# A gated feed-forward up projection by seven block products in place of eight, in a one-core decoder step

## The chip, the cores and the metric

The kernel runs as one program on one core of a Trainium2 chip. The metric is the device time of one execution, in microseconds. All matrix products are made in the format float32r from a high and a low part of each operand: a product of two matrices is three products on TensorE (high x high, high x low, low x high), accumulated in PSUM.

## The reference, cut to what matters

One layer of a decoder, for 1024 prompt tokens and 32 sample tokens with the same weights. The mixer has three branches (retention, a gated unit, attention into a memory); this case is about its last product and the feed-forward part behind it.

```python
merged = g_ret * (o_ret @ w_br_ret) + g_sg * (o_sg @ w_br_sg) + g_x * (o_x @ w_br_x)
x = x + merged @ w_o                                    # 1024 x 1024

z  = rmsnorm(x, norm_g) @ w_up                          # 1024 -> 2 * 2816
zp = concatenate([prev, z], axis=1)                     # two earlier tokens in front
zc = conv_b + sum(conv_w[j] * zp[:, j:j + L] for j in range(3))
a, b = split(zc, 2, axis=-1)
x = x + (gelu(a) * b) @ w_down                          # 2816 -> 1024
y = rmsnorm(x, norm_final_g)
```

The outputs beside y are states: of the retention, of the convolution (the last two rows of zp), the memory's keys and values.

## The kernel before, in words

All activations are kept with channels on the 128 partitions and the 1056 tokens (1024 and 32) along the free axis. A product's unit makes one tile of 128 output channels for all tokens: `fm` walks over 8 blocks of 128 input channels, and for each over three terms and three chunks of tokens (384, 384, 288), so 72 matmuls a unit, into one PSUM tile `mp` of three banks. There are two such tiles, and two single banks `ap`. SBUF is mostly a pool of 40 "slots" of 128 x 1056 float32.

Weights come as slabs of 128 x 1024 in the order of the list `SLABS`. `w_prep` takes a slab `wr`, lets ScalarE cast it to the high part `wh` and GpSimd subtract for the low part `wl`; two raw slabs and three prepared ones are there at a time, and `w_ahead` prepares the next one in the middle of a unit. `split` makes both parts of an activation in the same way (ScalarE casts, GpSimd, or VectorE, subtracts).

The order of all instructions is the order in which the program issues them (a manual schedule); each engine works through its own list in order, and the waits between engines come from the data, the slots and the PSUM banks. Work beside the matmuls is written as generators: `hook`, called after each block of input channels, takes a step of the first generator at a set rate, `drain` takes what is left, and `later` puts an instruction a few hooks off.

Around the change the order is: gates and branch products, then 8 units of the output product `("wo", m)`. After each, VectorE adds the residual x (`xres`), ScalarE and VectorE split the sum times the norm's gain into `hh` and `hl`, and GpSimd and VectorE add up the squares. The root of the norm (`rstd_all`, into `rst`) is not in these operands; it is multiplied in when the up product leaves PSUM:

```python
vtt(z[:, 2:770].rearrange("p (a b) -> p a b", a=2), ps[:, 0:2, 0:384],
    rst[:, 0:768].rearrange("p (a b) -> p a b", a=2), ALU.mult)
```

The 44 up units come in pairs (a row tile of a, `j`, and the one of b, `NFF + j`), two pairs a group. `conv` takes z out of PSUM and does the convolution: ScalarE the last tap and the bias, VectorE two multiply-adds; the 32 sample tokens have small instructions of their own. Then gelu of a on ScalarE, times b on VectorE, and `split` into `ach` and `acl`, which stay in SBUF. After each group of up units follow the down products of the group before (`down`): two input blocks, 8 output tiles, 144 matmuls, added to the residual `x2t` in SBUF. The last two groups are made by token chunks, and the final norm is worked in between them.

Of the kernel before, what the change touches and what calls it, by code (L numbers as in the profile page):

```python
# [8 lines left out]
F32 = mybir.dt.float32  # L9
# [5 lines left out]
P = 128  # L15
# [12 lines left out]
# products of (high, low) parts  # L28
# [14 lines left out]
def slab_order():  # L43
# [17 lines left out]
    o += [("wo", m) for m in range(8)]  # L61

    def up(g):
        r = []
        for j in (2 * g, 2 * g + 1):
            r += [("up", j), ("up", NFF + j)]
        return r

    dn = lambda g: [("dn", 2 * g), ("dn", 2 * g + 1)]
    o += up(0)  # L70
    for g in range(1, NFF // 2):
        o += up(g) + dn(g - 1)
    o += dn(NFF // 2 - 1)
# [4 lines left out]
# slabs whose low part is formed on the vector engine, the others on gpsimd  # L78
# [4 lines left out]
def step_kernel(ctx: ExitStack, tc: tile.TileContext, xT, memT, wslab, cst, ident_d, rope, vec, sgc, sgm, sgs,  # L83
# [49 lines left out]
    # ---------------------------------------------------------------- weights  # L133
    raws, hil, wst = {}, {}, {"d": 0, "p": 0, "live": 0}

    def w_dma():
        i = wst["d"]
        if i < len(SLABS) and i - wst["p"] < 2:
# [33 lines left out]
    def w_ahead():  # L172
        if wst["live"] < 3 and wst["p"] < len(SLABS) - 1:
            w_prep()

    # ------------------------------------------------------------------- aux
# [74 lines left out]
    def tm(keys, ops, evac, xsum):  # L251
        """token-major product with 256 weight columns, k in two slabs; xsum: scratch for the samples"""
# [45 lines left out]
    # --------------------------------------------------------------- norm  # L298
# [33 lines left out]
    def rstd_all(src):  # L332
        """as rstd_cols, for all tokens at once, into rst"""
# [20 lines left out]
    with tc.manual_schedule():  # L354
        # ------------------------------------------------ x, split with its gain
# [9 lines left out]
        # the first operands come in pieces, for an early start  # L365
# [43 lines left out]
        # the squares of the first half, and their sum  # L409
# [14 lines left out]
        # halves that the tanh forms of the sigmoids leave over  # L424
# [47 lines left out]
        # ------------------------------------------------------- retention  # L472
# [23 lines left out]
        def retention(h, qt, kt, silu, V, st, s3, s0, s0s):  # L496
# [34 lines left out]
            def A(p):  # L531
# [9 lines left out]
                # per token block: keys and scores, then, as float32r, their low parts  # L541
# [221 lines left out]
        # --------------------------------------------------- memory K and V  # L763
# [58 lines left out]
        # ------------------------------------------------ spatial gating unit  # L822
# [84 lines left out]
        # ---------------------------------------------------- cross-attention  # L907
# [172 lines left out]
        def reload(idx, dst):  # L1080
            """operands from DRAM, split again"""
# [46 lines left out]
        # ------------------------------------------------------------- merge  # L1128
# [73 lines left out]
        for m in range(8):  # L1202
# [3 lines left out]
            mops.append(split(acc[m], "mg"))  # L1206

        # ----------------------------------------------------- output product
        xres = {}

        def xload(m):
            if m < 8:
                xres[m] = slot("xres")
                dma(xres[m], xT[m])

        xload(0)
        xload(1)
        h2 = []
        ssq = slot("ssq")
        for m in range(8):  # L1220
            ps = fm(("wo", m), mops)
            x2 = xres.pop(m)
            for o, i in zip(seg(x2), psv(ps)):
                stt(o, i, 0.5, o, ALU.mult, ALU.add)
            hh, hl = slot("hh", F32R), slot("hl", F32R)
            g = vecs[:, VNF + m:VNF + m + 1]
            act(hh, x2, scale=g)
            stt(hl, x2, g, f(hh), ALU.mult, ALU.subtract)
            h2.append((hh, hl))
            dma(scx[m], x2)  # L1230
            if m == 0:
                ptt(ssq, x2, x2, ALU.mult)
            else:
                sq = slot("sq")
                ptt(sq, x2, x2, ALU.mult)
                vtt(ssq, ssq, sq, ALU.add)
            xload(m + 2)

        # --------------------------------------------------------------- FFN
        def fnorm():  # L1240
            for _ in range(3):
                yield
            yield from rstd_all(ssq)
            early["a"] = conv(0, early["ps"])

# [358 lines left out]
```

## Time and profile before

| | |
|---|---|
| median of 3 runs | 1984.75 us (1984.06 to 1984.93) |
| profiled execution: span from its first to its last instruction | 1984.1 us |
| mean granted TensorE clock | 0.992 |
| TensorE busy | 1928.9 us, 12455 matmuls |
| VectorE, ScalarE, GpSimd busy | 857.3, 537.8, 782.0 us |
| moved by DMA | 146.36 MB |

The profiled execution's own time isn't given apart from its span; the span lies within the runs. PE is TensorE's matmuls, PEld its weight loads, DVE VectorE, ACT ScalarE, POOL GpSimd, SP the queue that issues all DMAs here. Matmuls overlap in the pipeline, so a busy TensorE says little of how far apart its matmuls start. Every matmul has the line of the helper `mm` (L110), so groups are told apart by their tiles: `mp<-hh,wh` is a product into tile `mp` with the operands `hh` and `wh`.

### The profile page before, as it was taken

The numbers are of one execution on the slowest core, as the hardware profiler recorded it, in microseconds if no ns is written. First come the engines' busy times: TensorE is split into PE (matmuls) and PEld (weight loads), VectorE is DVE, ScalarE is ACT, GpSimd is POOL, SyncE is SP. The second block draws the span as 40 slices with busy tenths as digits, with TensorE's granted clock in tenths as the row PEclk, the third lists the DMA queues.
The fourth block names the chain that finished last, engine by engine and source line by source line (L and its number), as shares of the span: only waits on it lengthen the run. The fifth ranks groups of instructions, "written<-read, shape, count | busy, mean of one in ns | idle before, by whom it ended". The sixth has DMA issues, their size and how long they took to land.

```text
span 1984.1 us, 29054 instructions
## 1 busy us (share of the span) xinstructions
PE 1928.9 (97%) x12455; PEld 1905.1 (96%) x12455; DVE 857.3 (43%) x1318; ACT 537.8 (27%) x745; POOL 782.0 (39%) x572
## 2 busy tenths in 40 slices
PE   6999999999899999999999999999999999999997
PEld 6999999999899999999999999999999999999996
DVE  8463646442555532111112356444434434444456
ACT  5233222422134332111221213322222222222234
POOL 6242433231633334333353444433343343333343
PEclk9999999999999999999999999999999999999998
DMA  4112131314133322111221332311111111111112
GB/s 180 54 44 89 43 110 43 120 55 150 59 127 106 97 87 98 43 43 43 98 85 45 131 125 73 125 48 49 43 43 50 36 54 43 45 49 46 43 41 88
DMA packets 43088, 146.36 MB, mean 74 GB/s; under 512 B 4752, under 2 KB 7984, under 8 KB 42960
## 3 DMA queue, kind: packets, MB, share of 16 engines
q1 hardware_dynamic: 42960, 144.51, 20.8%
q8 instruction: 98, 1.61, 0.3%
q14 instruction: 30, 0.25, 0.0%
HBM read 120.95 MB, written 23.54 MB: 73 GB/s over the span
## 4 chain that ended last, share of the span: by engine, by line
PE 86%; DVE 7%; ACT 3%; issue 2%; DMA 1%; POOL 0%; SPq 0%; DVEq 0%; ACTq 0%; POOLq 0%
PE mp L110 81%; PE ap L110 4%; DVE hl L122 1%; DVE s L116 1%; DMA xr<-in_xT 1%; ACT sw L478 1%; DMA scr<-ox 0%; DVE ssf L116 0%; DVE rt L122 0%; DVE st L528 0%; PE ap L578 0%; DVE xr L116 0%; ACT th L113 0%; ACT xt L113 0%; DMA wr<-in_wslab 0%
## 5 line engine op out<-in xcount | busy, mean ns | idle before, releaser
L119 POOL TENSOR_TENSOR wl<-wr,wh 128x1024 fp32r<-128x1024 f32 x149 | 367.2, 2469 | 610.4 <-ACT wh L155 593.5
L110 PE MATMUL mp<-hh,wh 128*128 128x384 f32 (+1 forms) x2208 | 491.0, 330 | 10.3 <-ACT hh L113 5.5
L110 PE MATMUL mp<-hl,wh 128*128 128x384 f32 (+1 forms) x2208 | 481.3, 325 | 4.9 <-DVE hl L122 4.8
L110 PE MATMUL mp<-hh,wl 128*128 128x384 f32 (+1 forms) x2208 | 479.2, 324 | 0.0
L110 PEld LDWEIGHTS mp<-hh,wh 128*128 128x128 f32 x2208 | 366.2, 189 | 13.2 <-ACT hh L113 5.7
L110 PEld LDWEIGHTS mp<-hl,wh 128*128 128x128 f32 x2208 | 368.4, 189 | 7.5 <-DVE hl L122 7.5
L110 PEld LDWEIGHTS mp<-hh,wl 128*128 128x128 f32 x2208 | 368.1, 189 | 0.0
L155 ACT CAST wh<-wr 128x1024 fp32r<-128x1024 f32 x155 | 161.7, 1045 | 312.1 <-PE mp L110 286.4
L116 DVE TENSOR_TENSOR z<-mp,rst 128x768 f32<-128x768 f32 x88 | 56.7, 687 | 268.5 <-PE mp L110 268.4
L122 DVE SCALAR_TENSOR_TENSOR c<-z,hist,c 128x1024 f32<-128x1024 f32 x88 | 122.4, 1391 | 47.5 <-ACT c L113 41.7
L116 DVE TENSOR_TENSOR x<-x,mp 128x288 f32<-128x288 f32 (+3 forms) x167 | 105.7, 676 | 86.0 <-PE mp L110 86.0
L110 PE MATMUL mp<-acl,wh 128*128 128x384 f32 (+3 forms) x501 | 116.2, 325 | 0.0
L110 PE MATMUL mp<-ach,wh 128*128 128x384 f32 (+3 forms) x501 | 116.1, 325 | 0.0
L110 PE MATMUL mp<-ach,wl 128*128 128x384 f32 (+3 forms) x501 | 115.9, 324 | 0.0
L110 PE MATMUL mp<-wh,hl 128*128 128x256 f32 x384 | 108.1, 282 | 0.0
L110 PE MATMUL mp<-wh,hh 128*128 128x256 f32 x384 | 108.1, 282 | 0.0
L110 PE MATMUL mp<-wl,hh 128*128 128x256 f32 x384 | 108.0, 281 | 0.0
L116 DVE TENSOR_TENSOR th<-mp,rst 128x768 f32<-128x768 f32 (+1 forms) x48 | 31.6, 701 | 170.9 <-PE mp L110 150.3
L119 POOL TENSOR_TENSOR acl<-c,ach 128x1056 fp32r<-128x1056 f32 x21 | 51.8, 2467 | 127.1 <-ACT ach L294 127.1
L122 DVE SCALAR_TENSOR_TENSOR th<-th,mp 128x768 f32<-128x768 f32 (+1 forms) x48 | 31.6, 701 | 145.4 <-PE mp L110 145.4
L110 PEld LDWEIGHTS mp<-ach,wl 128*128 128x128 f32 x501 | 85.3, 189 | 1.1
L110 PEld LDWEIGHTS mp<-acl,wh 128*128 128x128 f32 x501 | 85.0, 189 | 1.1
(314 smaller groups left out, 2807.1 us busy)
## 6 DMA issues: line engine op xcount, KB each, us to landing
wr<-in_wslab SPq DMA_DIRECT2D x156, 512.0 KB, 3.5
opr<-scr SPq DMA_DIRECT2D x16, 528.0 KB, 5.6
scr<-ort SPq DMA_DIRECT2D x8, 528.0 KB, 7.6
xres<-in_xT SPq DMA_DIRECT2D x8, 528.0 KB, 4.3
scx<-xres SPq DMA_DIRECT2D x8, 528.0 KB, 3.0
x<-scx SPq DMA_DIRECT2D x8, 528.0 KB, 9.0
s<-in_sret SPq DMA_DIRECT2D x8, 512.0 KB, 5.9
out_srets<-s SPq DMA_DIRECT2D x8, 512.0 KB, 3.5
```

The lines of the kernel that those rows point to most:

```text
L110: nc.tensor.matmul(out=out, lhsT=l, rhs=r, start=start, stop=stop)
L116: nc.vector.tensor_tensor(out=out, in0=a, in1=b, op=op)
L119: nc.gpsimd.tensor_tensor(out=out, in0=a, in1=b, op=op)
L122: nc.vector.scalar_tensor_tensor(out=out, in0=a, scalar=s, in1=b, op0=op0, op1=op1)
L155: nc.scalar.copy(out=hi, in_=raw)
L478: nc.scalar.copy(out=o[a:a + 64], in_=i[b:b + 64])
```

## The change: what it does

The up product of pair j is seen as a product of 2 x 2 blocks. The weights are A11, A12 (the row tile of a, first and second half of the 1024 input channels) and A21, A22 (that of b); the operands B11, B12, B21, B22 are the two halves of the input channels and two halves of the tokens. A scheme with seven block products makes the four output blocks, with sums of weight blocks (s1 to s4, made for each pair) and sums of operand blocks (T1 to T4, made once):

```
s1 = A21 + A22   s2 = s1 - A11   s3 = A11 - A21   s4 = A12 - s2
T1 = B12 - B11   T3 = B22 - B12  T2 = B22 - T1    T4 = B21 - T2
P1 = A11 B11     r  = P1 + s2 T2     u3 = r + s3 T3     u4 = r + s1 T1
a, first half of the tokens:  P1 + A12 B21      second half:  u4 + s4 B22
b, first half of the tokens:  u3 + A22 T4       second half:  u3 + s1 T1
```

(T4 stands here with the sign that the code uses.) A block product has 4 blocks of input channels, three terms and two quarters of 264 tokens (256 and 8): 24 matmuls of 264 columns, into one of three sets of two banks, used in turn. Pair 0 is done with eight block products.

```diff
@@ slab order: the output product's slabs twice, up, then all of down
-    o += [("wo", m) for m in range(8)]
...
+    o += [("wo", m, s) for s in range(2) for m in range(8)]
+    for j in range(NFF):
+        o += [("up", j), ("up", NFF + j)]
+    o += [("dn", j) for j in range(NFF)]
@@ behind the branch products
+            mops.append(split_q(acc[m], "mg"))
+        for m in range(8):
+            x2c.append(slot("x2c"))
+            for o, i in zip(q_parts(x2c[m]), t_parts(xT[m])):
+                dma(o, i)
...
+        def half_norm(half, names, sub):
...
+            nc.scalar.copy(out=hi, in_=src)
+            vtt(lo, src, f(hi), ALU.subtract)
+            yield
+            for q in range(2):
...
+                mm(a, ones, hi[:, c], stop=False)
+                mm(a, ones, lo[:, c], start=False)
+                rstd_sum(a, r[:, c], t[:, c])
+            newton(r, t[:, 0:HW], t[:, HW:2 * HW])
+            for k in range(8):
+                g = vecs[:, VNF + k:VNF + k + 1]
+                stt(hs(k, half), hs(k, half), g, r, ALU.mult, ALU.mult)
+                x_split(names[k // 4], k % 4, hs(k, half), sub)
+                yield
@@ the output product: 2 halves of the tokens x 8 units
+        for half in range(2):
+            rate[0] = 0.25
+            for m in range(8):
...
+                            mm(ps[:, q, 0:QW], a[:, k, :], r[:, c0:c0 + QW], start=(k == 0 and i == 0),
+                               stop=(k == 7 and i == 2))
...
+                stt(o, ps[:, 0:2, 0:QW], 0.5, o, ALU.mult, ALU.add)
...
+                    act(sq[:, 0:HW], hs(m, half), AF.Square)
+                    vtt(s, s, sq[:, 0:HW], ALU.add)
+                for i, o in zip(q_parts(x2c[m]), t_parts(scx[m])):
+                    dma(o[:, 2 * half:2 * half + 2], i[:, 2 * half:2 * half + 2])
+            drain()
+            gens.append(half_norm(half, ("B11", "B21") if half == 0 else ("B12", "B22"), ptt if half == 0 else vtt))
@@ out of PSUM: a copy on ScalarE or an add on VectorE
+        def put(n, out, tmp=None):
+            for ps, q0 in banks[n]:
+                o = quarters(out)[:, q0:q0 + ps.shape[1]]
+                if tmp is None:
+                    nc.scalar.copy(out=o, in_=ps)
+                else:
+                    vtt(o, ps, quarters(tmp)[:, q0:q0 + ps.shape[1]], ALU.add)
@@ the weights of a pair, in steps
+        def f_prep(j):
...
+            def parts(names, src):
...
+                nc.scalar.copy(out=hi, in_=src)
+                ptt(lo, src, f(hi), ALU.subtract)
...
+            vtt(s1, a21, a22, ALU.add)
+            vtt(s2, s1, a11, ALU.subtract)
+            yield
+            ptt(s3, a11, a21, ALU.subtract)
+            ptt(s4, a12, s2, ALU.subtract)
+            yield
+            parts(("a11", "a12"), wa)
+            yield
+            t = slot("f22", F32R)
+            nc.scalar.copy(out=t[:, 0:512], in_=a22)
+            ptt(t[:, 512:1024], a22, f(t)[:, 0:512], ALU.subtract)
...
+            f_dma(j + 1)
+            yield
+            parts(("s2", "s3"), sa[:, 0:1024])
+            yield
+            parts(("s1", "s4"), sb[:, 0:1024])
+            yield
@@ sums of the operands, once, while pair 0's last two products run
+        def sums():
+            for k in range(4):
+                vtt(h(k, 0), h(k, 1), h(k, 0), ALU.subtract)
+                yield
+            for k in range(4):
+                ptt(h(k, 1), h(k + 4, 1), h(k, 1), ALU.subtract)
+                vtt(h(k + 4, 1), h(k + 4, 1), h(k, 0), ALU.subtract)
+                x_split("T2", k, h(k + 4, 1), vtt)
+                yield
+            for k in range(4):
+                x_split("T1", k, h(k, 0), ptt)
+                yield
+            for k in range(4):
+                ptt(h(k + 4, 0), h(k + 4, 0), h(k + 4, 1), ALU.subtract)
+                yield
...
+            for k in range(4):
+                x_split("T3", k, h(k, 1), ptt)
+                yield
+            for k in range(4):
+                x_split("T4", k, h(k + 4, 0), ptt)
+                yield
@@ pair 0, then pairs 1 to 21
+        for n, (r, half, bk) in enumerate(plan):
+            if n == 2:
+                drain()
+                gens.append(sums())
+                preps.append(f_prep(1))
+            for s in range(2):
+                prod([x[:, 512 * s:512 * s + 512] for x in wab[r]], f"B{s + 1}{half + 1}", bk, s == 0, s == 1, hook)
...
+        while preps:
+            turn(preps)
+            turn(convs)
...
+        for j in range(1, NFF):
...
+            d = fw.pop(j)
+            preps.append(f_prep(j + 1))
...
+            def after(n=1):
+                ticks()
+                for _ in range(n):
+                    turn(convs)
+                turn(preps)
...
+            n = prod(d["a11"], "B11")
+            put(n, p1)
+            after(2)
+            n = prod(d["s2"], "T2")
+            put(n, r, p1)
+            after()
+            n = prod(d["a12"], "B21")
+            za = z_new(j)
+            z_put(n, 0, *za, p1)
+            after()
+            n = prod(d["s3"], "T3")
+            put(n, u3, r)
+            after()
+            n = prod(d["s1"], "T1")
...
+            put(n, u4, r)
+            z_put(n, 1, *zb, u3)
+            after()
+            n = prod(d["s4"], "B22")
+            z_put(n, 1, *za, u4)
+            cell = []
+            convs.append(conv_a(j, *za, cell))
+            after()
+            n = prod(d["a22"], "T4")
+            z_put(n, 0, *zb, u3)
+            convs.append(conv_b(j, *zb, cell))
+            after(2)
+            while preps:
+                turn(preps)
@@ the activations go to DRAM, and come back for the down product
+            vtt(c, c, cell[0], ALU.mult)
+            later(2, lambda: dma(sca[j], c))
...
+        def a_load(j):
...
+                dma(oraw[j], sca[j])
+        def a_split(j):
...
+                acts[j] = split(oraw.pop(j), "ac", vtt if j == NFF - 1 else ptt)
@@ down, behind the whole loop
-                if m == 1:
+                if m in (1, 3, 5):
                     w_ahead()
-                step()
+                if m in (2, 4):
+                    a_split(2 * g + m // 2 + 1)
+                    a_load(2 * g + m // 2 + 3)
...
-        for g in range(1, G):
-            up(g)
-            if g <= G - FG:
-                down(g - 1)
...
+        for g in range(G - FG):
+            down(g)
```

So the kernel now has four stages here. The output product is made for the first half of the tokens and then for the second; each half is summed, squared, and brought by `half_norm` to its norm with gain and root and split (B11, B21 of the first half; B12, B22 of the second), the second half while pair 0 runs. `sums` and then the weights of pair 1 follow. The block loop runs over pairs 1 to 21: after each product a step of the convolutions (VectorE, ScalarE) and of the next pair's weights is issued. The gated activations are written to DRAM. The down product runs behind the loop on activations that are read back and split again; its last two groups and the final norm are as before.

More of the change, by code (lines that the diff above doesn't have):

```diff
@@ L172, in w_ahead @@
     def w_ahead():
-        if wst["live"] < 3 and wst["p"] < len(SLABS) - 1:
+        if wst["live"] < 3 and wst["p"] < min(wst["end"], len(SLABS) - 1):
             w_prep()
@@ L1205, in step_kernel @@
             vtt(acc[m], acc[m], tha[m], ALU.add)
[L1206 to L1218, printed above, removed]
-        ssq = slot("ssq")
[L1220 to L1244, printed above, removed]
-        gens.append(fnorm())
-        rate[0] = 1.0
-        coll = slot("coll", shape=[P, NUP, 18])
+            mops.append(split_q(acc[m], "mg"))
+        x2c = []
+        for m in range(8):
+            x2c.append(slot("x2c"))
+            for o, i in zip(q_parts(x2c[m]), t_parts(xT[m])):
+                dma(o, i)
+        ssq = slot("ssq")
         hsl = slot("hist")
@@ new lines, in step_kernel, with bank, prod @@
+        Bx, By = mp(), mp()
+        banks = {"a": [(Bx[:, 0:2, 0:QW], 0)], "b": [(By[:, 0:2, 0:QW], 0)],
+                 "c": [(Bx[:, 2:3, 0:QW], 0), (By[:, 2:3, 0:QW], 1)]}
+        def bank(n, q):
+            if n == "c":
+                return banks[n][q][0][:, 0, :]
+            return banks[n][0][0][:, q, :]
+        turns = [0]
+        def prod(w, name, n=None, start=True, stop=True, tick=None):
+            if n is None:
+                n = "abc"[turns[0] % 3]
+                turns[0] += 1
+            wh, wl = [x.rearrange("p (k c) -> p k c", c=P) for x in w]
+            for k in range(4):
+                xh, xl = xop(name, k)
+                for i, (a, r) in enumerate(((wh, xh), (wh, xl), (wl, xh))):
+                    for q in range(2):
+                        mm(bank(n, q), a[:, k, :], r[:, q * QW:(q + 1) * QW], start=(start and k == 0 and i == 0),
+                           stop=(stop and k == 3 and i == 2))
+                if tick:
+                    tick()
+            return n
@@ L1281, in conv @@
[L1281 to L1316 removed]
+            act(c[:, 0:TP], z[:, 2:1026], scale=w(2), bias=b)
@@ new lines, in step_kernel, with turn, ticks @@
+        convs, preps = deque(), deque()
+        def turn(q):
+            while q:
+                try:
+                    next(q[0])
+                    return True
+                except StopIteration:
+                    q.popleft()
+            return False
+        def ticks():
+            for e in wait:
+                e[0] -= 1
+            while wait and wait[0][0] <= 0:
+                wait.pop(0)[1]()
+        def sums():
+            h = hs
+            for k in range(4):
[12 more added lines that the diff above has]
+                yield
+            early["sums"] = True
+            for k in range(4):
+                x_split("T3", k, h(k, 1), ptt)
+                yield
+            for k in range(4):
+                x_split("T4", k, h(k + 4, 0), ptt)
+                yield
@@ new lines, in step_kernel @@
+        z0 = [z_new(0), z_new(NFF)]
+        rate[0] = 1.0
+        turns[0] = 1
+        wab = [w_get(("up", 0)), w_get(("up", NFF))]
+        cell = []
+        plan = [(0, 0, "a"), (1, 0, "b"), (0, 1, "c"), (1, 1, "a")]
+        f_dma(1)
+        for n, (r, half, bk) in enumerate(plan):
[5 more added lines that the diff above has]
+                prod([x[:, 512 * s:512 * s + 512] for x in wab[r]], f"B{s + 1}{half + 1}", bk, s == 0, s == 1, hook)
+                if n >= 2:
+                    for _ in range(3):
+                        step()
+                    if r == 1 and s == 0:
+                        w_free(("up", 0))
+            z_put(bk, half, *z0[r])
+            if n == 2:
+                convs.append(conv_a(0, *z0[0], cell))
@@ L1318, in dn_get @@
+        drain()
+        x2_load(range(8))
+        a_load(0)
+        a_load(1)
+        wst.update(d=FAST1, p=FAST1, live=0, end=len(SLABS))
+        w_dma()
+        w_dma()
+        a_split(0)
+        a_split(1)
+        a_load(2)
+        a_load(3)
+        while convs:
+            turn(convs)
         def dn_get(g):
```

195 lines of the change are left out of this document (132 added, 63 removed).

## The prediction

> **What bounds the kernel now.** I read the page first: how full each engine is, the slices, and the chain that ended last.
>
> ```profile
> span 1984.1 us, 29054 instructions
> PE 1928.9 (97%) x12455; PEld 1905.1 (96%) x12455; DVE 857.3 (43%) x1318; ACT 537.8 (27%) x745; POOL 782.0 (39%) x572
> PE   6999999999899999999999999999999999999997
> PE 86%; DVE 7%; ACT 3%; issue 2%; DMA 1%; POOL 0%; SPq 0%; DVEq 0%; ACTq 0%; POOLq 0%
> ```
>
> TensorE has work in every slice, the chain is 86% TensorE, and VectorE and GpSimd are busy about 40%. So the time goes with the pitch of the matmuls (start to start), and a wait on another engine costs only where it stops TensorE. The mean duration of a matmul is no pitch, since matmuls overlap. The pitch comes from the table of stretches (352 columns on average in the up and down products) and from the timeline (256 columns early, 512 late).
>
> ```profile
> core 0: us, PE busy (x) PEld busy (x) DVE busy (x) ACT busy (x) POOL busy (x), PEclk, DMA share, GB/s
> 1300.00:1400.00 100.00, 100.00 (x620) 100.00 (x619) 41.94 (x64) 23.62 (x25) 38.65 (x34) 1.00 0.14 48
> ...
> 74.86 0.28 PE L110 MATMUL mp<-wh,hl 128*128 128x256 f32 x1
> ...
> 78.89 0.28 PE L110 MATMUL mp<-wh,hh 128*128 128x256 f32 x1
> ...
> 1934.90 0.39 PE L110 MATMUL mp<-ach,wh 128*128 128x512 f32 x1
> ...
> 1939.54 0.40 PE L110 MATMUL mp<-acl,wh 128*128 128x512 f32 x1
> ```
>
> 100 us hold 620 matmuls: 161 ns. Between the two 256-column rows lie 34 pitches, 118.5 ns each; between the 512-column rows 20, 232 ns. The line through the last two is 5 ns + 0.443 ns a column; it gives 161 ns at 352, as seen, and **122 ns at 264**, the new width. Nothing suggests a step in between.
>
> Next, what the other engines pay for one instruction, from the answers for tiles c and wl and the groups by form (tiles: min/median/max ns; groups: busy us, mean ns).
>
> ```profile
> L122 DVE SCALAR_TENSOR_TENSOR c<-z,hist,c x88: 1270/1279/3547, 1219.2 to 1923.2; 128x1024 f32<-128x1024 f32 x88
> L122 DVE SCALAR_TENSOR_TENSOR c<-zs,hist,c x88: 235/240/2386, 1220.3 to 1924.4; 128x32 f32<-128x32 f32 x88
> L113 ACT ACTIVATE c<-z,hist x44: 1237/1246/1248, 1215.1 to 1918.3; 128x1024 f32<-128x1024 f32 x44
> L113 ACT ACTIVATE c<-zs,hist x44: 393/398/400, 1216.2 to 1919.4; 128x32 f32<-128x32 f32 x44
> L113 ACT ACTIVATE c<-c x22: 1086/1088/1090, 1222.0 to 1910.9; 128x1056 f32<-128x1056 f32 x22
> L116 DVE TENSOR_TENSOR c<-c x22: 1249/1257/1259, 1229.1 to 1924.7; 128x1056 f32<-128x1056 f32 x22
> L119 POOL TENSOR_TENSOR wl<-wr,wh x149: 2330/2406/3432, 34.9 to 1917.5; 128x1024 fp32r<-128x1024 f32 x149
> ...
> L119 POOL TENSOR_TENSOR vg<-vg,sgW 128x512 f32<-128x512 f32 x8 | 10.3, 1292 | 5.8 <-DVE vg L876 4.4 <-ACT vg L113 0.7 <-issue 0.7
> L116 DVE TENSOR_TENSOR ssf<-ssf,sq 128x512 f32<-128x512 f32 x7 | 4.8, 691 | 0.6
> L116 DVE TENSOR_TENSOR x<-x,mp 128x512 f32<-128x512 f32 x8 | 5.1, 684 | 4.7 <-PE mp L110 4.7
> L116 DVE TENSOR_TENSOR zs<-mp,rst 128x32 f32<-128x32 f32 x44 | 8.0, 181 | 0.0
> L155 ACT CAST wh<-wr 128x1024 fp32r<-128x1024 f32 x155 | 161.7, 1045 | 312.1 <-PE mp L110 286.4 <-issue 20.6 <-DMA wr<-in_wslab 4.8
> L113 ACT ACTIVATE sq<-x 128x512 f32<-128x512 f32 x7 | 4.3, 632 | 2.4 <-DVE x L116 2.4
> ```
>
> The maxima (3547 for a multiply-add of 1279) have one cause, which the timeline shows:
>
> ```profile
> 13.76 18.95 DVE L122 SCALAR_TENSOR_TENSOR hl<-xr,vecs,hh 128x1056 fp32r<-128x1056 f32 x6
> ...
> 12.71 18.89 POOL L119 TENSOR_TENSOR xr<-xr 128x1056 f32<-128x1056 f32 x6 [3.18 <-DVE hl L122]
> ...
> 1919.63 1.38 DVE L122 SCALAR_TENSOR_TENSOR c<-z,hist,c 128x1024 f32<-128x1024 f32 x1 [1.41 <-ACT c L113]
> 1920.94 2.39 DVE L122 SCALAR_TENSOR_TENSOR c<-zs,hist,c 128x32 f32<-128x32 f32 x1
> ...
> 1919.88 3.39 POOL L119 TENSOR_TENSOR wls<-wr,whs 128x1024 fp32r<-128x1024 f32 x1
> ...
> 1395.30 1.50 DVE L122 SCALAR_TENSOR_TENSOR c<-z,hist,c 128x1024 f32<-128x1024 f32 x1 [1.28 <-ACT c L113]
> ...
> 1393.31 2.40 POOL L119 TENSOR_TENSOR wl<-wr,wh 128x1024 fp32r<-128x1024 f32 x1 [7.70 <-ACT wh L155]
> ...
> 1404.29 1.29 DVE L116 TENSOR_TENSOR z<-mp,rst 128x768 f32<-128x768 f32 x2 [5.97 <-PE mp L110]
> ...
> 1404.98 2.40 POOL L119 TENSOR_TENSOR wl<-wr,wh 128x1024 fp32r<-128x1024 f32 x1 [6.76 <-ACT wh L155]
> ```
>
> A VectorE instruction with two SBUF inputs and a GpSimd one that reads SBUF take turns. Six of each, 1.25 and 1.95 to 2.4 us alone, need 19 us, their sum. At 1919.88 the low part waits out the multiply-add (3.39 for 2.41), then the 32-column one (0.24 alone) waits 2.1 us for it. Whoever waits goes next. An add with one input in PSUM (1404.29) is not held and holds nobody.
>
> **The change part by part.** The sum stands on this execution, span 1984.1; the runs lie between 1984.06 and 1984.93, so their median is 0.65 above it and little lies around the span.
>
> *Matmuls of the block loop.* Per pair of up rows 144 matmuls at 161 ns (23.2 us) become 7 products of 24 at 122 ns: 2.93 us each, 20.5 in all. For 21 pairs: **-57 us**. Pair 0 keeps 8 products (192 x 122 ns = 23.4): +0.2.
>
> *Output product.* 576 matmuls at 161 ns become 768 at 122: +1.0. Eight more weight slabs (DMA on SP's queue, ACT cast 1.05, GpSimd 2.41 in each 5.86 us unit) and SP's 16 loads and 32 stores in pieces are hidden by the slabs already ahead. The first unit, though, reaches the last input block after 7/8 of 5.86 = 5.1 us instead of 10.2, and that block's low part is late:
>
> ```profile
> L110 PE MATMUL mp<-mgh,wh x192: 292/336/343, 1100.1 to 1192.0; 128*128 128x384 f32 x128, 128*128 128x288 f32 x64
> ...
> 1104.20 2.47 POOL L119 TENSOR_TENSOR mgl<-th,mgh 128x1056 fp32r<-128x1056 f32 x1 [6.81 <-ACT mgh L294]
> ```
>
> It ends 6.6 us after the first matmul, about 6.9 with the added small pieces: +1.8.
>
> *Block loop, other engines.* Per pair GpSimd gets two sums of 512 (1.29 each), three low parts (2.41), half a one (1.2) and small copies (0.4, an estimate): 11.4 us. VectorE gets two sums (0.69), four multiply-adds (1.27), four small ones (0.24), a product (1.26): 8.7 us. These take turns: **20.1 us of 20.5**. Seven adds out of PSUM (0.69, and 0.18 for the samples, 5.6 us) run beside them. VectorE's queue is in order, and a PSUM bank set comes back after three products, so each add must be done within two products of its own. The tightest path runs from the end of product 7 to the add after product 2 of the next pair, which product 5 waits for: add 0.96, two convolution steps 2.86, gelu 1.09, ACT's next convolution 1.25, step 1.43, weight sums 1.38, add 0.70, hand-overs 0.2: 9.9 us of 4 x 2.93 = 11.7. Slack 1.8. On the way stand the low part of s1 and s4 (issued one product earlier; 2.4, of which the row at 1395.30 shows 0.2 overlapped) and perhaps s3's sum (1.2): 2.2 to 3.4 us, so 0.4 to 1.6 of stall. A second place is the add after product 3, queued behind the second convolution step, which may wait for s4's sum and the low part of a11 and a12: 0 to 2.1. Bounds 0 and 3.8 a pair; I take 1.5, as the two places seldom hit in one pair: **+31** (0 to +80).
>
> The Trainium skill, "SBUF — State Buffer", section "Who interferes with whom", has the later of the two fully blocked until the first finishes, and lets adds out of PSUM go free. The trace agrees, but for the 0.2 us of start-up: 1.50 instead of 1.27 with 0.42 us of overlap. By the page alone some six hand-overs a pair would cost up to 1.2 us more, 2046 instead of 2021 below.
>
> *Entry to the loop.* Before, the root of the norm was applied late, on the product. Now it must be in the operands. Counted from the last output matmul: add 0.75, square 0.65, sum 0.7, cast 0.65, low part 0.7 is 3.5, while TensorE meets the ones-product after one block step, 1.5: **+2**. Root, mean square and Newton step are priced by these rows of today's root:
>
> ```profile
> 1202.32 1.28 ACT L113 ACT_TABLE_LOAD   x1
> ...
> 1204.13 0.58 ACT L113 ACTIVATE rst<-ap,epst 128x384 f32<-128x384 f32 x1 [0.53 <-PE ap L110]
> 1204.74 0.56 DVE L311 TENSOR_SCALAR rms<-ap 128x384 f32<-128x384 f32 x1 [1.15 <-ACT rst L113]
> ```
>
> 1.28, twice about 0.45 and 0.4, three steps of 0.7: 5. Then each of 8 blocks needs 0.7 + 0.65 + 0.7 in VectorE's order, 2.1: done at 25.2. Pair 0's first two products end at 13.7, the third would end at 19.6 and can't before 26: **+6**. It ends the fourth at 32. Only then may the block sums run, and they stand in GpSimd's queue ahead of pair 1's weights: 20 GpSimd instructions of 528 (1.27, from 1.29 for 512 down to 1.2, half of 2.41), 25.4 us, taking turns with 12 of VectorE (0.7, 8.5 us); then pair 1's sums (1.4 and 2.5), the first low part (2.4). 25.2 + 40.2 is 65, plus one convolution step of pair 0 (1.5): 67. TensorE waits from 32 to 67: **+35**. Were nothing to take turns, the GpSimd work alone (30.3 from 26) would end at 56: +24. These are the bounds, with 40 if two more steps get between. The second product waits for s2's low part, 2 more: +2. No transfer fills this; TensorE has nothing else.
>
> *Exit.* After the last product: add 1.0, two steps 2.9, gelu 1.1, ACT's convolution with copies 2.1, then in ACT's queue the first down slab's cast 1.05 (8 us), its low part 2.4 plus a turn 0.5: 10.9; the second slab's low part costs 2 more: **+12** (8 to 14). The 22 stores and loads of the activations (528 KB) have two pairs or a group of time.
>
> *Down, apart.* With three slab buffers the fourth cast waits for the last row's first half; cast 1.05 and low part 2.41 end some 0.3 us after they are wanted, 8 times: +2.5 (0 to 6). Activations' low parts: two a group, 2.47 each of 23.2 us, hidden.
>
> *The clock and the end.*
>
> ```profile
> 1925.00:1931.00 6.00, 4.72 (x21) 3.53 (x20) 2.31 (x3) 2.57 (x3) 0.00 (x0) 1.00 0.17 68
> ...
> 1970.00:1984.10 14.10, 3.03 (x16) 1.98 (x14) 7.96 (x16) 2.42 (x6) 4.43 (x5) 0.73 0.40 137
> ```
>
> The wait for the last activation before the final groups (6.00 less 4.72) goes: -1. Where TensorE idles, the granted clock falls (0.73); after two long waits I take 1 us each: +2 (0 to 4). The Trainium skill, "TensorE: Matmul & The Clock Gate", Part 1, halves the clock after about 3.4 us of idling for about that long, which would be 1.7 each; this row fits a fall but not its length.
>
> **Sum.** -57 + 0.2 + 1.0 + 1.8 + 31 + 2 + 6 + 35 + 2 + 12 + 2.5 - 1 + 2 = +37.5, so 1984.1 + 37.5 = 2021.6; I say **2021**.
>
> **The rivals.**
> (a) *Faster: the two engines don't hold each other* in instructions of half the width. Then the loop runs at TensorE's pace (0 for 31), and the entry waits 24 and 1 instead of 35 and 2, the exit 9.5 for 12: 37.5 - 31 - 11 - 1 - 2.5 = -8, 1976. It decides where all waits together fall below 57 us. For it: their sum of busy shares is only 82% now. Against: the rows at 13.76, with turns taken throughout. 0.12.
> (b) *They hold each other, yet the loop keeps TensorE's pace*, since 20.1 is below 20.5 and the banks give slack: 0 for 31, 1990. For it: every wait in a bound I could not order for sure. Against: slack 1.8 with 2.2 on the path. 0.2.
> (c) *Both places hit in every pair*: 24.3 us a pair, more than the 23.2 of before: +80 for 31, 2070. 0.12.
> (d) *It doesn't do what it says*: 264 columns cost the old 161 ns, 27 us a pair. Then 21 x 6.5 is 137, less the 31 that it would hide: 2127. The 118.5 ns at 256 speak against it: 0.02.
>
> **How the numbers follow.** My case (1 to 2 us of stall a pair, 2010 to 2032) gets 0.54. For eight times in ten I reach below (b) to 1981, which leaves out (a), and up to 2070, which leaves out half of (c), and (d). 0.2% of 1984, 4 us, is about what a measurement of this kernel can tell from no change. Faster: (a), 0.12. Same: the lower edge of (b), 0.04. Slower: 0.84.
>
> **What would show it.** Right: 264-column matmuls 122 ns apart; TensorE idle some 35 us before the first block product, released by GpSimd's wl, while GpSimd has no gap; multiply-adds in the loop longer than 1.28; products released by VectorE's adds; 8 us or more of idling before the first down matmul. Wrong: a loop of 20.5 us a pair without idle TensorE, GpSimd and VectorE overlapping freely, or a table of stretches in which the entry idles under 20 us.

## The result and the profile after

| | before | after |
|---|---|---|
| median of the runs | 1984.84 us (1984.06 to 1987.44) | 2203.12 us (2201.65 to 2205.39) |
| ratio, 95% interval | | 1.1095 (1.1079 to 1.1111) |
| span of the profiled execution | 1984.1 us | 2199.9 us |

The kernel is 218 us slower; the forecast was 37 us slower, 2021 us, with 2070 us as the upper end. First the page of the changed kernel. In its lines `vtt` is now L112 (an add on VectorE), `stt` L118 (a multiply-add), `ptt` L115 (GpSimd), `mm` L106; L1343 and L1358 are the copies out of PSUM on ScalarE, L1420 the cast of a pair's weights, L151 that of a slab.

```profile
span 2199.9 us, 31595 instructions
PE 1947.7 (89%) x13201; PEld 1896.7 (86%) x13201; DVE 1024.9 (47%) x1576; ACT 617.9 (28%) x971; POOL 939.6 (43%) x604
PE   7999999998999999999999377787777877699997
PEclk9999999999999999999999699998998999899998
PE 18%; DVE 10%; issue 8%; POOL 2%; ACT 2%; DMA 1%; DVEq 0%; SPq 0%; POOLq 0%; ACTq 0%
```

TensorE's tenths fall to 3 in slice 23, the entry that was expected, and then stay at 7 or 8 for the 11 slices of the block loop, which was expected to run at 9. The view of waits says who holds TensorE (total us, times, longest):

```profile
PE mp L106 <- DVE zt L112: 76.6, 21, 4.8
PE mp L106 <- DVE zs L112: 54.1, 56, 2.3
PE mp L106 <- ACT zs L1358: 18.0, 3, 8.9
PE mp L106 <- POOL wl L115: 13.6, 11, 8.0
```

The first row is 21 waits, one in each pair, of 3.65 us on average, for `zt`, the tile of r = P1 + s2 T2. The second is almost three shorter ones a pair. The timeline of one pair shows the first, TensorE and then VectorE and ScalarE (start, duration, instruction, idle time before it and its releaser):

```profile
1506.68 0.40 PE L106 MATMUL mp<-xh,f 128*128 128x264 f32 x2
...
1508.23 0.41 PE L106 MATMUL mp<-xh,wl 128*128 128x264 f32 x2
...
1513.33 0.41 PE L106 MATMUL mp<-xh,wl 128*128 128x264 f32 x2
1513.57 0.28 PE L106 MATMUL mp<-xh,wh 128*128 128x264 f32 x1
1518.57 0.59 PE L106 MATMUL mp<-xh,wh 128*128 128x264 f32 x1 [4.71 <-DVE zt L112]
1518.95 0.64 PE L106 MATMUL mp<-xl,wh 128*128 128x264 f32 x2
...
1522.91 0.48 PE L106 MATMUL mp<-xl,wh 128*128 128x264 f32 x2
```
```profile
1507.82 2.39 DVE L118 SCALAR_TENSOR_TENSOR c<-z,hist,c 128x1024 f32<-128x1024 f32 x1
1510.13 1.27 DVE L118 SCALAR_TENSOR_TENSOR c<-zs,hist,c 128x32 f32<-128x32 f32 x1
1511.33 1.27 DVE L118 SCALAR_TENSOR_TENSOR c<-z,hist,c 128x1024 f32<-128x1024 f32 x1
...
1515.12 1.28 DVE L118 SCALAR_TENSOR_TENSOR c<-z,hist,c 128x1024 f32<-128x1024 f32 x1 [2.35 <-ACT c L109]
...
1516.48 0.69 DVE L112 TENSOR_TENSOR fs<-wr 128x512 f32<-128x512 f32 x1
1517.20 0.69 DVE L112 TENSOR_TENSOR fs<-fs,wr 128x512 f32<-128x512 f32 x1
1517.81 0.70 DVE L112 TENSOR_TENSOR zt<-mp,zt 128x528 f32<-128x528 f32 x1
```
```profile
1512.80 1.09 ACT L109 ACTIVATE c<-c 128x1056 f32<-128x1056 f32 x1 [1.30 <-DVE c L118]
1513.79 1.23 ACT L109 ACTIVATE c<-z,hist 128x1024 f32<-128x1024 f32 x1
```

Three things are to be read here.

- The pitch is as forecast: 22 pair rows from 1508.23 to 1513.33 are 42 pitches, 121 ns each (122 forecast). Seven products at that pace are 20.5 us.
- VectorE's list is the forecast path, and it is nearly as long as forecast: product 7 ends at 1507.1, the add of r at 1518.5, 11.4 us later. The forecast had 9.9 us of work and 2.2 to 3.4 for turns, together 12.1 to 13.3. Two of the turns are in the 2.39 and the 1.27 us (1.27 and 0.24 alone).
- But TensorE stops at 1513.6, right behind product 2, and the matmul at 1518.57 is the first of **product 3**. The forecast had product 5 wait for this add. And it starts at half pace: 18 pitches from 1518.95 to 1522.91, 220 ns each. This lasts 4.4 us and costs another 2.0.

Over the loop the distances between matmul starts hold 167.7 us of waits, and the matmuls at half pace add about 44 us, together 10.1 us a pair: 20.5 + 10.1 = 30.6 us, and the gelus of pairs 1 and 21 lie 20 x 30.5 us apart. The forecast had 22.0. 21 pairs x 8.5 us is 179 us, and the spans differ from the sum (2021.6) by 178. So the miss lies in the loop alone.

Why product 3? These lines give out PSUM in the changed kernel; `mp()` is a tile of three banks:

```python
Bx, By = mp(), mp()
banks = {"a": [(Bx[:, 0:2, 0:QW], 0)], "b": [(By[:, 0:2, 0:QW], 0)],
         "c": [(Bx[:, 2:3, 0:QW], 0), (By[:, 2:3, 0:QW], 1)]}
```

Set c is the third bank of the two tiles that also hold a and b. If the waits between matmuls and the instructions that empty PSUM go by tile and not by bank, a product in c waits until b (just before it) is emptied, and one in a until c is. Then two of three products wait for the add directly before them, and the three sets are worth hardly more than one. This is theory A. It can be tried on this trace: the sets are taken in turn, and a pair has seven products, so product 3 lies in a, b and c in three pairs one after another. A product in b shares its tile with c alone and need not wait for the add directly before it. In the 14 pairs in which product 3 lies in a or c, product 3 waits for the add of r, as above; in the 7 pairs in which it lies in b (2, 5, 8 and so on), product 3 runs on, and product 4, in c, waits for it: 2.0 us, and 2.3 us more for the add of product 3, one matmul later. Theory B: the sets don't matter; the order in VectorE's queue and the turns with GpSimd set it.

### The profile page after: what moved, and what is told of

The parts are those of the page before. It is cut to its first block, busy times and chain, and to the rows that moved or that the text cites. A ratio compares the mean times of both kernels' runs of the same rounds, so it can differ in the third digit from the quotient of the medians.

```text
span 2199.9 us, 31595 instructions
## 1 busy us (share of the span) xinstructions
PE 1947.7 (89%) x13201; PEld 1896.7 (86%) x13201; DVE 1024.9 (47%) x1576; ACT 617.9 (28%) x971; POOL 939.6 (43%) x604
## 5 line engine op out<-in xcount | busy, mean ns | idle before, releaser
L115 POOL TENSOR_TENSOR wl<-wr,wh 128x1024 fp32r<-128x1024 f32 x136 | 344.2, 2536 | 568.2 <-ACT wh L151 493.9
L106 PE MATMUL mp<-xh,wh 128*128 128x264 f32 x1072 | 252.1, 312 | 164.9 <-DVE zt L112 76.6
L106 PEld LDWEIGHTS mp<-xh,wh 128*128 128x128 f32 x1072 | 186.0, 207 | 185.2 <-DVE zt L112 81.0
L106 PE MATMUL mp<-hh,wh 128*128 128x384 f32 (+1 forms) x1152 | 263.4, 336 | 9.8 <-ACT hh L109 4.9
L106 PE MATMUL mp<-hl,wh 128*128 128x384 f32 (+1 forms) x1152 | 253.6, 328 | 4.8 <-DVE hl L118 4.8
L106 PE MATMUL mp<-hh,wl 128*128 128x384 f32 (+1 forms) x1152 | 251.3, 325 | 0.0
L106 PE MATMUL mp<-xh,wl 128*128 128x264 f32 x1072 | 233.8, 302 | 8.0 <-POOL wl L115 8.0
L106 PE MATMUL mp<-xl,wh 128*128 128x264 f32 x1072 | 234.1, 302 | 0.0
L106 PEld LDWEIGHTS mp<-hh,wh 128*128 128x128 f32 x1152 | 192.4, 191 | 12.6 <-ACT rsh L352 5.1
L106 PEld LDWEIGHTS mp<-hl,wh 128*128 128x128 f32 x1152 | 193.1, 190 | 7.2 <-DVE hl L118 7.2
L151 ACT CAST wh<-wr 128x1024 fp32r<-128x1024 f32 x121 | 125.9, 1043 | 253.7 <-PE mp L106 221.2
L106 PEld LDWEIGHTS mp<-hh,wl 128*128 128x128 f32 x1152 | 193.3, 190 | 0.0
L106 PEld LDWEIGHTS mp<-xh,wl 128*128 128x128 f32 x1072 | 182.6, 206 | 8.3 <-POOL wl L115 8.3
L118 DVE SCALAR_TENSOR_TENSOR c<-z,hist,c 128x1024 f32<-128x1024 f32 x88 | 164.0, 1864 | 54.8 <-ACT c L109 54.8
L106 PEld LDWEIGHTS mp<-xl,wh 128*128 128x128 f32 x1072 | 183.0, 207 | 0.0
L112 DVE TENSOR_TENSOR x<-x,mp 128x288 f32<-128x288 f32 (+3 forms) x167 | 105.8, 676 | 132.0 <-PE mp L106 132.0
L115 POOL TENSOR_TENSOR wl<-fs,wh 128x1024 fp32r<-128x1024 f32 x42 | 101.0, 2405 | 148.9 <-ACT wh L1420 148.9
L106 PE MATMUL mp<-ach,wh 128*128 128x384 f32 (+3 forms) x501 | 117.4, 328 | 9.8 <-ACT wh L151 9.8
L106 PE MATMUL mp<-ach,wl 128*128 128x384 f32 (+3 forms) x501 | 117.9, 329 | 5.6 <-POOL wl L115 5.6
L106 PE MATMUL mp<-acl,wh 128*128 128x384 f32 (+3 forms) x501 | 117.2, 327 | 0.0
L112 DVE TENSOR_TENSOR th<-mp,rst 128x768 f32<-128x768 f32 (+1 forms) x48 | 31.7, 701 | 170.9 <-PE mp L106 150.3
L106 PE MATMUL mp<-wh,hl 128*128 128x256 f32 x384 | 108.1, 282 | 0.0
```

The source lines that it names most:

```text
L106: nc.tensor.matmul(out=out, lhsT=l, rhs=r, start=start, stop=stop)
L112: nc.vector.tensor_tensor(out=out, in0=a, in1=b, op=op)
L115: nc.gpsimd.tensor_tensor(out=out, in0=a, in1=b, op=op)
L118: nc.vector.scalar_tensor_tensor(out=out, in0=a, scalar=s, in1=b, op0=op0, op1=op1)
L151: nc.scalar.copy(out=hi, in_=raw)
```

## Experiments: what holds the loop

Each kernel is the changed one with the edit shown. Single times stand beside a run of the kernel before of 1985.1 to 1987.6 us on the same chip. All edits but the last were run once, and the ten runs of the last one spread over 5.3 us; gains of 5 or 7 us below are therefore read from the waits as well as from the time.

**Set c in tiles of its own** (the two single banks `ap`, free in the loop).

```diff
+                banks["c"] = [(ap().rearrange("p (o c) -> p o c", o=1)[:, :, 0:QW], q) for q in range(2)]
```

> The third set of PSUM banks gets two tiles of its own (the two single banks), in place of the third banks of the tiles that hold the other two sets; nothing else changes. Theory A (sets that share a tile wait for each other, so every second or third product waits for the evacuation just before it, and the add after product 2 stops product 3 instead of product 5): that add comes 11.7 us after product 7 and is then needed at 11.7, so a pair takes 21 to 22.5 us instead of 30.5; total 2015 to 2040. Rival B (VectorE's queue and its turns with GpSimd need 30 us a pair whatever the banks): over 2150. Rival C (half the effect: the sharing costs its four or five short waits, the long one stays): 2090 to 2120.

Measured: 2021.91 us, 21.7 us a pair. The row of 400 us in the loop from the table of stretches (length, busy time of PE, PEld, DVE, ACT and POOL, granted clock, DMA share, GB/s), then the same kernel's waits for the add of r:

```profile
1300.00:1700.00 400.00, 386.06 (x3098) 380.08 (x3099) 335.71 (x475) 155.30 (x261) 251.07 (x188) 1.00 0.25 74
```
```profile
PE mp L106 <- DVE zt L112: 11.1, 13, 0.9
...
PE ap L106 <- DVE zt L112: 3.5, 6, 0.6
```

No instruction is taken away, none is moved in any queue, and 181 us are gone. Theory A holds; B can't explain it. The granted clock is 1.00 in this row, so the half pace went with the long waits; the changed kernel has 0.92 in 600 us of its loop:

```profile
1300.00:1900.00 600.00, 461.08 (x3288) 440.32 (x3287) 328.16 (x501) 166.09 (x277) 266.57 (x193) 0.92 0.17 54
```

What is left is a wait of up to 0.9 us for r in 19 of the 21 pairs, before the start of product 5, where the forecast had it. One of them, and what the two engines that take turns do in the meantime:

```profile
1417.29 0.41 PE L106 MATMUL mp<-xh,f 128*128 128x264 f32 x2
...
1430.26 0.51 PE L106 MATMUL mp<-xh,wh 128*128 128x264 f32 x2 [0.88 <-DVE zt L112]
```
```profile
1426.82 1.29 DVE L118 SCALAR_TENSOR_TENSOR c<-z,hist,c 128x1024 f32<-128x1024 f32 x1 [2.36 <-ACT c L109]
...
1429.51 0.70 DVE L112 TENSOR_TENSOR zt<-mp,zt 128x528 f32<-128x528 f32 x1
```
```profile
1429.67 1.28 POOL L115 TENSOR_TENSOR fs<-wr,fs 128x512 f32<-128x512 f32 x1 [6.46 <-DVE fs L112]
```

Product 7 ends at 1417.7 and the add of r at 1430.2: the path takes 12.5 us here, more than the 11.7 that four products leave it. Products 5 to 7 then take 9.2, and 12.5 + 9.2 is the pair of 21.7.

**The second convolution step behind the add of r**, tiles shared as in the change.

```diff
-            after(2)
+            after()
```

> Shared tiles as they are; after product 1 of each pair only one step of the convolutions is issued instead of two, so that the add after product 2 stands ahead of b's first multiply-add, which waits for gelu and ScalarE, in VectorE's queue. Theory A: the long wait of 4.7 us and the half clock behind it (2 us) go, four to five waits of 0.5 to 1.5 us a pair stay: 24.5 to 26.5 us a pair, total 2075 to 2120. Rival B (turns at the port set the time): no change beyond 2 us a pair, 2160 to 2205.

Measured: 2111.49 us, 26.0 us a pair. The waits for `zt` fall, those for `zs` (the adds that empty the sets) stay:

```profile
PE mp L106 <- DVE zs L112: 46.5, 56, 3.5
...
PE mp L106 <- DVE zt L112: 15.4, 14, 3.4
```

**Without the convolution's multiply-adds**, tiles shared (the 176 multiply-adds are left out of the computation).

> Leaves out the two earlier taps of the convolution (all 176 multiply-adds on VectorE): 6 of VectorE's 14.3 us a pair, and most of what takes turns with GpSimd. Shared tiles as they are. Theory A: what is left is the sharing alone, 4.7 waits a pair of an add and its hand-over, 0.8 to 1 us: 24 to 25.5 us a pair, total 2065 to 2100. Rival B: with the port free the loop runs at TensorE's 20.5 to 21.5 us, total 1990 to 2015.

Measured: 2084.85 us, 24.9 us a pair. VectorE is busy 163.41 of the 400 us from 1300 on, 10.2 us a pair where the changed kernel has 16.7, and still the pair is 4.4 us longer than TensorE's 20.5. Both results lie where theory A put them: a shorter list ahead of an add shortens the wait, but two of three products still wait for the add before them.

**What sets the remaining 21.7 us?** Both edits again, now with set c in its own tiles. Theory D: the time of the instructions that take turns (20.1 us in the forecast) fills the pair. Theory E: only the order ahead of the add of r. (The second expectation gives the letter E to another rival, the matmuls or the banks.)

> Both: own tiles for the third set and the add after product 2 ahead of the multiply-add. Theory A: no product waits for an add any more, 20.5 to 21.2 us a pair, total 1995 to 2015, what is left above 1927 being the entry (45 us) and the exit (12). Rival B: over 2100. If the turns at the port cost more than the order saves, it lies above the run with own tiles alone.

> Own tiles for the third set, and the two earlier taps of the convolution left out (176 multiply-adds on VectorE). With own tiles a pair still took 21.7 us, 1.2 more than its matmuls. Theory D (what is left is the port that VectorE's two-input instructions and GpSimd share, and the queue behind it): without the taps the loop falls to TensorE's 20.4 to 20.7 us a pair; total 1990 to 2002. Rival E (what is left has to do with the matmuls or the banks): 21.5 or more a pair, 2015 to 2022.

Measured: 2022.79 us, 21.7 us a pair, for the order (a miss, 1995 to 2015 was expected); 1993.54 us, 20.5 us a pair, without the multiply-adds. With the order changed, TensorE's waits only change their place, to `zs`, the last adds of the pair:

```profile
PE mp L106 <- DVE zs L112: 12.4, 12, 1.2
...
PE ap L106 <- DVE zs L112: 5.5, 6, 0.9
```

So neither E stands: not the order alone, and not the matmuls or the banks, which the second kernel leaves as they are. The order puts another limit of about the same length in the place of the first. VectorE, busy 335.71 of 400 us with own tiles alone (84%), now works without a pause (339.15 of 350 us, 97%), and its whole list, with the time in which GpSimd holds it up, is what a pair takes:

```profile
1350.00:1700.00 350.00, 334.22 (x2698) 330.23 (x2696) 339.15 (x413) 135.58 (x230) 231.47 (x160) 1.00 0.21 71
```

**The running sum of the convolution in PSUM.** Leaving work out shows no cause for sure, since it also shortens VectorE's list. This edit leaves all work and all queues in order, and only takes one of the two SBUF inputs from the four long multiply-adds of a pair:

```diff
-            act(c[:, 0:TP], z[:, 2:1026], scale=w(2), bias=b)
+            cv = lpp.tile([P, 2, 512], F32, tag="mc", name="cv", bufs=1)
+            act(cv, tap(2), scale=w(2), bias=b)
...
-                stt(c[:, 0:TP], z[:, j:j + TP], w(j), c[:, 0:TP], ALU.mult, ALU.add)
+                stt(cv if j else c[:, 0:TP].rearrange("p (a b) -> p a b", a=2), tap(j), w(j), cv, ALU.mult, ALU.add)
```

(`tap(j)` is z from column j on. For `cv` the two tiles of three banks become tiles of two in the loop.)

> Set c in tiles of its own, and the running sum of the convolution stays in a PSUM tile between its taps: ACT writes the first tap there, and the four 1024-column multiply-adds of VectorE in a pair have one input in PSUM, so that by the rows of the adds out of PSUM they take no turns with GpSimd. The order of both queues is unchanged. Theory D (the instructions that take turns, 20.1 us a pair in the prediction, set the 21.7 us of the loop with own tiles): these fall by 4 x 1.27 = 5.1 us to 15 us a pair, and a pair takes 20.4 to 20.9 us (TensorE's own 20.5): 21 x 1.0 = 21 us and up to 5 at the entry less than 2021.9, 1995 to 2008. Rival F (VectorE's queue in its own order sets it, whoever takes turns): the multiply-adds are no shorter, a pair stays above 21.5 us, 2015 to 2022.

Measured: 1995.48 us, 20.6 us a pair, at the lower end of what theory D gave. The long multiply-adds, by tile (min/median/max ns), with own tiles and then with the sum in PSUM:

```profile
L118 DVE SCALAR_TENSOR_TENSOR c<-z,hist,c x88: 1271/1287/3434, 1250.2 to 1738.6; 128x1024 f32<-128x1024 f32 x88
```
```profile
L118 DVE SCALAR_TENSOR_TENSOR cv<-z,hist,cv x44: 1277/1284/1291, 1249.8 to 1708.5; 128x1024 f32<-128x1024 f32 x44
L118 DVE SCALAR_TENSOR_TENSOR c<-z,hist,cv x44: 1267/1270/1275, 1252.3 to 1709.9; 128x1024 f32<-128x1024 f32 x44
```

None of the 88 takes longer than 1291 ns now, and between 1400 and 1500 us no two matmuls start more than 0.3 us apart. The Trainium skill, "SBUF — State Buffer", "Who interferes with whom", lets an instruction with at most one SBUF input go free; these rows agree. The path from product 7 (ends at 1407.4) to the add of r (1417.8) takes 10.4 us instead of 12.5, less than the 11.7 that there are. So F falls: the same work in the same order takes 1.1 us a pair less once the long multiply-adds take no turns. Theory D is borne out in that, but not in its wording that the turns *fill* the pair: with own tiles neither VectorE nor GpSimd works from 1424.5 to 1426.8, in the rows above, while VectorE waits for ScalarE. What the traces show is that the turns lengthen VectorE's list, and with it the path to the add of r.

## Experiments: the two ends of the loop

All with set c in its own tiles. **The exit**: the first two down slabs and activations are brought, cast and split during the last pair, instead of behind it: the DMAs after its product 3, the first slab and activation after 5, the second after 6.

```diff
+            if last:
+                exit_ahead(3)
...
+                exit_ahead(5)
...
+                exit_ahead(6)
...
-        a_load(0)
-        a_load(1)
...
-        a_split(1)
```

> Own tiles, and the first two down slabs and the first two activations are loaded and split during the last pair, where GpSimd has nothing, instead of behind the last convolutions. Theory: the exit's idle 15.2 + 2.5 us with own tiles is the row of ScalarE and GpSimd work behind the last product; 12 to 17 us go, total 2005 to 2010. Rival (the activations' way through DRAM sets the exit): under 4 us go.

Measured: 2014.78 us, 7 us gained, less than expected (2005 to 2010). The waits at the exit, with own tiles and then with this edit:

```profile
1735.39 1.25 PE L106 MATMUL mp<-ach,wh 128*128 128x384 f32 x3 [14.91 <-ACT wh L151]
...
1738.70 1.25 PE L106 MATMUL mp<-ach,wl 128*128 128x384 f32 x3 [2.07 <-POOL wl L115]
```
```profile
1722.55 0.76 PE L106 MATMUL mp<-ach,wl 128*128 128x384 f32 x3 [0.77 <-POOL wl L115]
...
1725.90 1.25 PE L106 MATMUL mp<-acl,wh 128*128 128x384 f32 x3 [2.59 <-DVE c L118]
...
1737.16 1.22 PE L106 MATMUL mp<-ach,wh 128*128 128x384 f32 x3 [4.90 <-DVE x L112]
```

TensorE starts the down product at once and then waits for VectorE, which has the last convolution to finish: 17.0 us of waits became 8.3.

**The entry**: pair 1's weights are prepared while pair 0 runs (its sums s1 and s2 on GpSimd), T3 is split ahead of T1, T4 last, and pair 1 makes A12 B21 ahead of s2 T2.

```diff
-                x_split("T1", k, h(k, 0), ptt)
+                x_split("T3", k, h(k, 1), ptt)
...
+            if n == 0:
+                preps.append(f_prep(1))
...
+            if j == 1:
+                n = prod(d["s2"], "T2")
```

> Own tiles, and three changes of order at the entry: pair 1's weight sums and first low parts are issued during pair 0's first two products (its sums on GpSimd), T3's split ahead of T1's and T4's behind pair 0, and pair 1 makes a12 x B21 ahead of s2 x T2. No work is left out. Theory (the entry's 46 us are GpSimd's and VectorE's turns on the sums, with pair 1's weights behind them in the queue): 20 to 30 us of idling go, total 1992 to 2002. Rival (the entry's idling is the norm and the split of the second half, 14 us of it, and the rest can't be overlapped): under 10 go.

Measured: 2016.93 us, 5 us gained (1992 to 2002 was expected). The first loop product ends 33 us earlier than with own tiles (1236.6 against 1269.8). But the next three products of pair 1 wait 6.09, 2.93 + 7.41 and 3.49 us, the pair's last product ends at 1280.6 against 1287.6, 7 us earlier, and its gelu comes at 1289.3 against 1294.2, only 5 us earlier. The work that takes turns was moved from ahead of pair 1 into it, and most of what was won is waited for there. **Both ends together**:

> Own tiles, with the changed order at the entry and at the exit together. If the two add up: 1977 to 1990, near the kernel before (1985); what is left above 1927 is the loop's 1.2 us a pair (25), the rest of the entry (20) and small waits (8).

Measured: 2011.12 us (1977 to 1990 was expected): 11 us, about the sum of the two.

**All of it**: own tiles, the sum in PSUM, entry and exit.

> The kernel with tiles of its own for set c and the running sum in PSUM, together with the two changes tried at the ends: the first two down slabs and activations brought and split during the last pair, and pair 1's weights, T3 and the first product with s2 taken in another order at the entry. Theory D: what the entry's change won and lost again in pairs 1 and 2 stays won when the loop has room (12 to 15 us), the exit's change gives the 7 us that it gave before, so about 20 us below the kernel with the running sum in PSUM alone: 1975 to 1990, about the kernel before the change. Rival F: as the two changes together without it, 2005 to 2012.

Measured in 10 runs: 1982.44 us, ratio to the kernel before 0.9983 (0.9974 to 0.9993). With room in the turns the entry's edit keeps more of what it wins (pair 1's gelu comes at 1279.9 against 1288.6 with the sum in PSUM alone, 8.6 us earlier). The two waits at the entry with the sum in PSUM alone, and the four with all edits:

```profile
1252.36 0.81 PE L106 MATMUL mp<-xh,wh 128*128 128x264 f32 x2 [22.37 <-ACT wh L1423]
...
1262.15 0.81 PE L106 MATMUL mp<-xh,wl 128*128 128x264 f32 x2 [8.54 <-POOL wl L115]
```
```profile
1240.60 0.93 PE L106 MATMUL ap<-xh,wh 128*128 128x264 f32 x2 [6.06 <-ACT zs L1359]
...
1248.33 0.81 PE L106 MATMUL mp<-xh,wh 128*128 128x264 f32 x2 [2.90 <-ACT wh L1423]
...
1254.06 0.81 PE L106 MATMUL mp<-xh,wl 128*128 128x264 f32 x2 [4.49 <-POOL wl L115]
...
1264.06 0.90 PE L106 MATMUL ap<-xh,wh 128*128 128x264 f32 x2 [2.71 <-DVE zs L112]
...
1697.50 1.22 PE L106 MATMUL mp<-ach,wh 128*128 128x384 f32 x3 [10.52 <-DVE c L118]
```

At the exit this kernel waits 10.52 us for the last multiply-add, which now reads PSUM that the down product's tiles take over (this reason is argued from the code and was not tried apart; with the sum in PSUM alone the first down product waits for the same instruction, 15.80 us). So this version ends 0.17% below the kernel before, at the edge of what can be told from no change: of the 21 x 2.6 = 55 us that its loop saves (20.6 a pair for 23.2) most are spent at the two ends. From the last output matmul to the end of pair 21 it takes 490.5 us, where pair 0 and 21 pairs of 20.6 need 456: 34 us for the entry; the exit's 10.5 and the half pace behind it are some 12.

## Why the prediction was wrong, point by point

- **The step that failed** is the sentence "a PSUM bank set comes back after three products, so each add must be done within two products of its own". It counted banks; the waits go by tiles. With c in the tiles of a and b, the add after product 2 has to be done before product 3 (in every third pair before product 4), not before product 5: two products less, 5.9 us (or one, 2.9). That wait and the shorter ones for the other adds make 8.0 us a pair, where the sum had 1.5, in bounds of 0 and 3.8. With this undone by one line the time is 2021.91 us; 2021 was forecast.
- **The stall at half pace was not in the sum.** The forecast took 1 us for each of two long waits of the whole kernel. The Trainium skill, "TensorE: Matmul & The Clock Gate", Part 1, which it weighed beside that, gave 1.7: about 3.4 us of idling, then half the clock for about as long. The trace is nearer to the page: 4.4 us of half pace behind the 4.7 us wait above, 2.0 us lost. But 3.4 us of idling are not needed here: the wait ahead of the matmul at 1884.77, in pair 21, is 2.3 us long and is followed by a granted clock of 0.50 from 1885.0 to 1888.3. What was missing in the sum is that such waits come in every pair: about 44 us.
- **Right: the pitch** (121 against 122 ns) and so the 57 us of matmuls saved; with own tiles and the sum in PSUM a pair takes 20.6.
- **Right in the main: the turns of VectorE and GpSimd.** The path from product 7 to the add of r, forecast at 12.1 to 13.3 us, took 11.4 in the changed kernel and 12.5 with own tiles, where a pair takes 21.7 us and the forecast had 22.0. The first of its two places shows (up to 0.9 us before product 5, 0.4 to 1.6 forecast), the second, the add after product 3, does not. What the forecast did not see is the limit behind it: with the path relieved by another order the pair stays at 21.7, as VectorE's list is then full. Only fewer turns made it shorter, by 1.1 us.
- **Right: the entry.** The last output matmul ends at 1195.6; nine products of 2.93 us would end at 1221.9, and the first loop product ended at 1266.9: 45 us late, and 2 + 6 + 35 + 2 were forecast. It splits otherwise than forecast. The 18.0 us behind `ACT zs` in the list of waits are pair 0's products; with own tiles these waits are gone, but the waits for the first loop weights are 22.4 and 12.5 us in place of the 9.05 and 8.02 below (34.9, close to the forecast's 35). The block sums and weights set the end either way.

```profile
1235.92 0.81 PE L106 MATMUL mp<-xh,wh 128*128 128x264 f32 x2 [8.89 <-ACT zs L1358]
...
1252.78 0.81 PE L106 MATMUL mp<-xh,wh 128*128 128x264 f32 x2 [9.05 <-ACT wh L1420]
...
1262.05 0.81 PE L106 MATMUL mp<-xh,wl 128*128 128x264 f32 x2 [8.02 <-POOL wl L115]
```

- **Right: the exit and the first output unit.** 9.77 and 2.06 us of waits against 12, and 1.17 us against 1.8:

```profile
1104.63 0.51 PE L106 MATMUL mp<-mgl,wh 128*128 128x264 f32 x2 [1.17 <-POOL mgl L115]
...
1913.88 1.25 PE L106 MATMUL mp<-ach,wh 128*128 128x384 f32 x3 [9.77 <-ACT wh L151]
...
1917.19 1.25 PE L106 MATMUL mp<-ach,wl 128*128 128x384 f32 x3 [2.06 <-POOL wl L115]
```

- That the kernel with own tiles meets the 2021 so closely is partly luck: its loop is 6 us shorter than forecast and its exit, 17.0 us of waits, 5 longer.
- **The rivals**: (a) is refuted, the two engines do hold each other (2.39 us for a multiply-add of 1.27 in the timeline above). The loop at TensorE's pace, which (b) had, came only after the turns were relieved. (c), 24.3 us a pair, was the largest stall that the forecast allowed for, and the true 30.5 lay outside it, since every bound was made with the same count of banks. (d) was wrong.

## What to carry to other kernels

Count how far ahead TensorE may run by the tiles that the waits go by, not by the banks that are free: one buffer cut from the spare ends of two others ties all three together (30.5 against 21.7 us a pair here). Where VectorE and GpSimd take turns, add the turns to each path on which TensorE waits for VectorE (12.5 us with them here, 10.4 with fewer, and 11.7 at hand), and look for an input that can stay in PSUM as well as for a better order: with own tiles the order alone moved nothing. And when a stretch of such work is moved to relieve one wait, ask whether it only waits in another place.

## What the runs showed of the hardware

- Whether matmuls fell to half pace did not go by the length of one wait alone. With the second convolution step moved, the loop has six waits of 1.9 us: behind three of them the matmuls kept 0.12 us, behind the other three they fell to 0.22 us after 1.2 to 1.6 us (granted clock 0.50 from 1439.0 to 1442.4, for one). Waits of 3.4 us and more in the loop, there and in the changed kernel, were all followed by 0.22 us a matmul, for 3 to 5 us in most cases. The wait of 4.7 us shown above so cost 43% more than its length.
- A long multiply-add with one of its two big inputs in PSUM took 1267 to 1291 ns beside GpSimd's low parts, as an add out of PSUM does, where the form with both in SBUF went up to 3434.
- With own tiles VectorE was busy 18.2 us a pair (335.71 of 400 us), and by the forecast's rows its work alone is 14.3 (8.7 and 5.6): by this estimate GpSimd holds it for 3.9 us in each pair.
